# Normalising half of the input in a layout with channels on partitions, in place of transposing it

## The chip, the cores and the metric

The kernel runs on one core of a Trainium2 chip. The metric is the device time of one launch in microseconds (us); of several runs the median is given. Everything is float32; matrix products take a value as a rounded high part and the remainder (float32r tiles `hi` and `lo`) and add three products.

## The reference

One layer of an encoder over 2048 tokens of 1024 channels (D). Cut to what matters here:

```python
def _layernorm(x):
    xf = x.astype(jnp.float32)
    mu = jnp.mean(xf, axis=-1, keepdims=True)
    var = jnp.mean(jnp.square(xf - mu), axis=-1, keepdims=True)
    return (xf - mu) * lax.rsqrt(var + LN_EPS)

mod = c_act @ ada_w[l] + ada_b[l]
shift, scale, gate = jnp.split(mod, 3, axis=-1)
h = (_layernorm(x) * (1.0 + scale[:, None, :]) + shift[:, None, :]).astype(x.dtype)
proj = h @ w_in[l]                       # 1024 -> 9216 columns
y_hg = ...                               # gated recurrence (HGRN2), 8 heads, both directions
y_na = ...                               # 2-D neighbourhood attention, 16 heads, times a gate
y = jnp.concatenate([y_hg, y_na], axis=-1) @ w_out[l]
z = DEEPNORM_ALPHA * x + gate[:, None, :] * y
x = (_layernorm(z) * ln_g[l] + ln_b[l]).astype(x.dtype)
```

The matrix products need h with channels on the partitions; mean and variance of a token go over its channels.

## The kernel before

The tokens are cut in two halves of 1024 and each half in two groups of 512 (`GRP`): groups 0 and 1, then 2 and 3. h of one half lies in SBUF as 32 tiles `h` of 128 channels by 512 tokens (8 channel blocks `k`, two groups, high and low part). The h of the second half (`hs`, in DRAM) is prepared while the first half is worked on, and loaded over the first (`reload`, line 1429) when that is done.

The stages in order: `startup` (modulation sums, groups 0 and 1, first projections); `first_half` (neighbourhood attention of the first half, pair of heads by pair, in 8 rounds w); the recurrence, 16 rounds over heads and halves; the attention of the second half; the output projection with the final normalisation. In each stage `weave` mixes a generator of attention or recurrence steps with a generator `dense` of projection matmuls (`proj_mm`, line 272; `vproj`, line 285), so that TensorE has dense work between the dependent steps. A round of `first_half` holds, in TensorE's order: sums over values (line 1122), scores (1054, 1058), dense matmuls, transposes of the shares (1103), dense matmuls. VectorE and ScalarE do the softmax (1071 to 1081) between scores and transposes, and split each weight block into high and low part (842, 843).

In `first_half` TensorE's instructions keep the order in which the program writes them. Those of VectorE, ScalarE and SP are put in order by a planner at compile time, by priority and by when it estimates that operands and buffers are ready; each engine then runs its list strictly in that order, waiting where an operand is late. `pinned` keeps chosen instructions in the program's order among themselves (the statistics, line 212, are pinned). A tile of a tag has a fixed number of buffers, and a new tile waits for the last use of the old one: in this stage the tag `x` has 8 and the tag `s` (`short()`) 3.

Work on groups 2 and 3 (g = 0 and 1 in `first_half`) is put into `slots`, four for a round, which `natten_woven` calls between its steps. `rows` loads the 512 tokens as 8 tiles x of 128 tokens by 512 channels (line 199). `stats` takes mean and variance (212, 213) and the rate 1/sqrt(var + eps) (`rstd_of`, 184 to 191). `scale` normalises the tiles in place, half on ScalarE (226), half on VectorE (228). Each of 8 `piece`s then transposes four 128x128 blocks on TensorE into a PSUM tile (line 233, in `h_piece`), applies the modulation on ScalarE (235), takes high and low part on VectorE (239, 240) and stores both to `hs` (1345, 1346). The slots before and after:

```python
for g, i in ((0, 10), (1, 21)):
    slots[i].append((rows, g))
    slots[i + 1].append((stats, g))
    slots[i + 2].append((scale, g, 0))
    slots[i + 3].append((scale, g, 1))
    for k in range(KT):
        slots[i + 3 + k].append((piece, g, k))
```

All DMAs of this stage are issued by the queue of SP: weight blocks (line 832), key mirrors (987), value tiles (1000), bias tables (735, 736), stores (293, 1015, 1017, 1133), tables of the bias (718, 719). Earlier in the stage `gate_sum` stores 128 x 8 single elements to `gate_d` (line 178).

Of the kernel before, what the change touches and what calls it, by code (L numbers as in the profile page):

```python
# [10 lines left out]
F32 = mybir.dt.float32  # L11
F32R = mybir.dt.float32r
U32 = mybir.dt.uint32
AF = mybir.ActivationFunctionType
ALU = mybir.AluOpType
PSUM = bass.MemoryType.PSUM

D = 1024
SEQ = 2048
P = 128  # L20
KT = D // P
HALF = 1024
GRP = 512
# [14 lines left out]
def body(ctx: ExitStack, tc: tile.TileContext, t):  # L38
    nc = tc.nc
    dve, act, pool, pe = nc.vector, nc.scalar, nc.gpsimd, nc.tensor  # L40
    dma = nc.sync.dma_start
    x, out = t["x"], t["out"]

    cp = ctx.enter_context(tc.tile_pool(name="cp", bufs=1))
# [19 lines left out]
    def dram(name, shape, dt=F32):  # L64
        if name in t:
            return t[name]
        return nc.dram_tensor(name, shape, dt, kind="Internal").ap()
# [2 lines left out]
    yT = [yq[i // 4][:, i % 4, :] for i in range(16)]  # L70
    gate_d = dram("gate_d", (8, P))
    c_d = dram("c_d", (D,))
    hs = [dram(f"hs{k}", (P, 2, HALF)) for k in range(KT)]
    op_d = [dram(f"op{i}", (P, HALF)) for i in range(NHEAD)]
    qb_d = [dram(f"qb{i}", (P, HALF)) for i in range(NHEAD)]
# [15 lines left out]
    def nm(s):  # L91
        cnt[0] += 1
        return f"{s}_{cnt[0]}"

    def tl(tag, dt=F32, shape=None):
        if tag in cur["smap"]:
            tag = cur["smap"][tag]
            return sh.tile([P, 512], dt, tag=tag, name=nm(tag), bufs=SH[tag])
        return cur["pool"].tile([P, 512] if shape is None else shape, dt, tag=tag, name=nm(tag), bufs=cur["bufs"].get(tag, 1))

    def short(dt=F32):
        return tl("s", dt)

    def ps(tag="mx"):
        if tag == "pj":
            return pp.tile([P, 512], F32, tag=tag, name=nm("pj"))
        tag = cur["map"].get(tag, tag)
        return cur["psum"].tile([P, 512], F32, tag=tag, name=nm("ps"), bufs=cur["ps"][tag])
# [17 lines left out]
    shift = cp.tile([P, KT], F32, name="shift")  # L126
    scale1 = cp.tile([P, KT], F32, name="scale1")
# [65 lines left out]
    def x_load(g, pre=None):  # L193
        xs = []
        for i in range(4):
            xt = [pre if pre and i == 0 else tl("x"), tl("x")]
            r0 = g * GRP + i * P
            for a in range(2):
                dma(xt[a], x[r0:r0 + P, a * 512:(a + 1) * 512])
            xs.append(xt)  # L200
        return xs

    def x_stats(xs, pin=lambda x: x):
        mv = cp.tile([P, 4, 2], F32, tag="xmv", name=nm("xmv"), bufs=2)
        for i in range(4):
            x_stat(xs[i], mv[:, i, :], pin)
        return x_rate(mv)

    def x_stat(xt, mv, pin=lambda x: x):
        st = cp.tile([P, 2, 6], F32, tag="bnst", name=nm("bnst"), bufs=4)  # L210
        for a in range(2):
            pin(dve.bn_stats(st[:, a, :], xt[a]))
        dve.bn_aggr(mv, st)

    def x_rate(mv):
        r = cp.tile([P, 4], F32, tag="xr", name=nm("xr"), bufs=2)
        rstd_of(r, mv[:, :, 1])
        b = cp.tile([P, 4], F32, tag="xb", name=nm("xb"), bufs=2)
        dve.scalar_tensor_tensor(b, mv[:, :, 0], -1.0, r, op0=ALU.mult, op1=ALU.mult)
        return mv, r, b  # L220

    def x_scale(xs, how, a, on_act=2):
        mv, r, b = how
        for i in range(4):
            if i < on_act:
                act.activation(xs[i][a], xs[i][a], AF.Identity, scale=r[:, i:i + 1], bias=b[:, i:i + 1])
            else:
                dve.tensor_scalar(xs[i][a], xs[i][a], mv[:, i, 0:1], r[:, i:i + 1], op0=ALU.subtract, op1=ALU.mult)

    def h_piece(xs, k, hi, lo, early=False):  # L230
        pt = ps("hx")
        for i in range(4):
            pe.transpose(pt[:, i * P:(i + 1) * P], xs[i][k // 4][:, (k % 4) * P:(k % 4 + 1) * P], ident)
        tmp = short()
        act.activation(tmp, pt, AF.Identity, scale=scale1[:, k:k + 1], bias=shift[:, k:k + 1])
        if early:
            act.activation(hi, tmp, AF.Copy)  # L237
            return lambda: dve.tensor_tensor(lo, tmp, hi, op=ALU.subtract)
        dve.tensor_copy(hi, tmp)
        dve.tensor_tensor(lo, tmp, hi, op=ALU.subtract)  # L240
# [1073 lines left out]
    def first_half(raws, feed):  # L1314

        st = Prep(0, 0, raws)
        for n, _ in NCOL0:
            for g in range(2):
                st.piece(n, g)
        for _ in range(2):  # L1320
            feed.free(0)
        feed.tick()
        for j in (0, 1, 3):
            st.table("top", j)
        for _ in vproj(t["w_v"][0], nv_d[0], 0, feed):
            feed.tick()
        for c in range(3):
            st.v(c)
        pipe, xs = [], {}

        def rows(g):
            xs[g] = x_load(2 + g)

        how = {}

        def stats(g):
            how[g] = x_stats(xs[g], pinned)

        def scale(g, a):
            x_scale(xs[g], how[g], a)  # L1340

        def piece(g, k):
            a, b = short(F32R), short(F32R)
            h_piece(xs[g], k, a, b)
            dma(hs[k][:, 0, g * GRP:(g + 1) * GRP], a.bitcast(F32))
            dma(hs[k][:, 1, g * GRP:(g + 1) * GRP], b.bitcast(F32))

        slots = {i: [] for i in range(32)}
        slots[0].append((bias_pair, 1))
        for m in range(8):  # L1350
            slots[1 + m].append((gate_load, m))
            slots[3 + m].append((gate_sum, m))
        slots[5].append((lower_bounds,))
        for g, i in ((0, 10), (1, 21)):
            slots[i].append((rows, g))
            slots[i + 1].append((stats, g))
            slots[i + 2].append((scale, g, 0))
            slots[i + 3].append((scale, g, 1))
            for k in range(KT):
                slots[i + 3 + k].append((piece, g, k))  # L1360
        for u in range(2, 8):
            slots[4 * u - 6].append((bias_pair, u))
        for w in range(8):
            extra = {i: slots[4 * w + i] for i in range(4)}
            if w < 7:
                nxt = Prep(w + 1, 0, {n: [None, None] for n, _ in NCOL})
                dense, total, steps = first_stream(nxt, feed), NLEN + (0 if w % 2 == 0 else VLEN), 8
            else:
                nxt, dense, total, steps = None, hgrn_dense(0, 0, feed=feed), HTOT, 9
            r = weave(natten_woven(st, nxt, pipe, extra, w == 7), dense, total, steps)[1]  # L1370
            st = nxt
        return r
# [45 lines left out]
    with tc.manual_schedule(engines={mybir.EngineType.PE}):  # L1418
        with psum_phase("st", *SPS), phase("st", SB_, SMS), tc.manual_schedule(engines={getattr(mybir.EngineType, e) for e in ("PE", "SP", "Activation", "DVE")}):
            raws, feed = startup()  # L1420
        with psum_phase("n0", *NPS0), phase("n0", NB0, SM0):
            natten_init(4, 0)
            st = first_half(raws, feed)
# [232 lines left out]
def _arrays(inp):  # L1656
    import numpy as np

    f = {k: np.asarray(v) for k, v in inp.items()}
    a = {}  # L1660
    a["x"] = f["x"].reshape(SEQ, D)
    a["c"] = f["c"].reshape(P, KT)
    a["ada_w"] = f["ada_w"].reshape(D, 24, P).transpose(1, 2, 0)
    a["ada_b"] = f["ada_b"].reshape(24, P).T
    a["w_in"] = f["w_in"].reshape(KT, P, 72, P).transpose(2, 1, 0, 3).reshape(72, P, D)
    for n, c in (("w_i", 1024), ("w_v", 7168)):
        a[n] = f["w_in"].reshape(KT, P, 9216)[:, :, c:c + 1024].reshape(KT, P, 4, 256).transpose(2, 1, 0, 3).reshape(4, P, 2048)
    a["lb_logits"] = f["lb_logits"].reshape(16, P).T
    a["hg_norm_g"] = f["hg_norm_g"].reshape(P, 1)
    a["rpb"] = f["rpb"].reshape(2, 120, 31)  # L1670
    a["w_out"] = f["w_out"].reshape(2 * D, D)
    a["ln_g"] = f["ln_g"].reshape(1, D)
    a["ln_b"] = f["ln_b"].reshape(1, D)
    i, j = np.arange(P)[:, None] % 32, np.arange(32)[None, :]
    off, low, fw = i // 16 != j // 16, i < 16, i <= j
    a["mskd"] = np.stack([off, ~off & np.where(low, i >= j, fw), ~off & np.where(low, fw, i >= j)], 1).astype(np.float32)
    return {k: np.ascontiguousarray(v) for k, v in a.items()}
# [16 lines left out]
```

## Time and profile before

| | |
|---|---|
| median of 3 runs | 2611.91 us (2610.88 to 2613.2) |
| the profiled execution, its own time | 2614.25 us |
| span from its first to its last instruction | 2612.5 us |
| mean granted TensorE clock | 0.998 |
| instructions | 46055 |
| DMA traffic | 352.84 MB, 135 GB/s in the mean |

The profile is of one execution, taken by the hardware. PE is TensorE's matmuls and PEld its weight loads, which overlap them; DVE is VectorE, ACT ScalarE, POOL GpSimd, SP the engine whose queue (SPq) issues the DMAs. L233 is line 233. A row of instructions says what is written and read (`ps<-ident,x`: PSUM tile from identity and x), with buffer numbers left out. In the chain of work that ended last, each entry is a start, a length and a place; the engine named there had no slack in that time. The ends of matmuls are modelled, so lengths of neighbouring matmuls overlap; starts are measured.

### The profile page before, as it was taken

The page shows a single profiled execution, that of the slowest core. Times are in us where ns is not written, and L with a number is a line of the kernel's source. Part 1 is how long each engine was busy: PE and PEld are TensorE (multiplying, and loading weights), DVE is VectorE, ACT ScalarE, POOL GpSimd, SP SyncE. Part 2 cuts the span into 40 slices and gives each one's busy share as a digit, 9 for nine tenths or more (in the row PEclk, how much of TensorE's full clock was granted, in tenths as well). Part 3 has the DMA queues.
Part 4 walks back from the last instruction along what each step waited for, and adds up shares of the span by engine and source line. Part 5 has one row for each costly group of instructions (what it writes and reads, how often), then busy time and mean ns, then how long its engine had stood idle before and what let it go on. Part 6 is the DMA issues. An engine that isn't in the chain of part 4 may idle for free.

```text
span 2612.5 us, 46055 instructions
## 1 busy us (share of the span) xinstructions
PE 2565.1 (98%) x17328; PEld 2147.1 (82%) x17328; DVE 1756.1 (67%) x4351; ACT 1417.6 (54%) x2808; POOL 98.2 (4%) x119
## 2 busy tenths in 40 slices
PE   5999999999999999999999999999999999999998
PEld 3888888888888888888888888898888878888887
DVE  6446445478777778877787788537788888658443
ACT  4434444376666667666676666446666667531110
POOL 0000000000000000000000000000000000032221
PEclk9999999999999999999999999999999999999999
DMA  7555454212353347433233222454554445544331
GB/s 263 171 171 157 137 180 140 102 66 94 85 150 132 118 135 265 156 123 127 85 108 99 74 77 75 124 179 146 166 173 144 139 142 184 186 149 129 97 97 57
DMA packets 246318, 352.84 MB, mean 135 GB/s; under 512 B 31831, under 2 KB 122199, under 8 KB 245463
## 3 DMA queue, kind: packets, MB, share of 16 engines
q1 hardware_dynamic: 245807, 349.37, 42.3%
q8 instruction: 136, 2.23, 0.4%
q14 instruction: 87, 0.71, 0.1%
q10 hardware_dynamic: 288, 0.53, 0.1%
HBM read 266.21 MB, written 113.39 MB: 145 GB/s over the span
## 4 chain that ended last, share of the span: by engine, by line
PE 92%; DVE 3%; DMA 3%; ACT 2%; issue 1%; SPq 0%; DVEq 0%; ACTq 0%
PE pj L272 51%; PE pj L285 6%; PE ps L1510 4%; PE ps L1512 4%; PE ps L1511 4%; PE ps L1122 4%; PE ps L1103 3%; PE ps L486 2%; PE ps L1054 2%; PE ps L478 2%; PE ps L553 1%; PE ps L1058 1%; PE ps L577 1%; PE ps L579 1%; PE ps L525 1%; PE ps L654 1%
## 5 line engine op out<-in xcount | busy, mean ns | idle before, releaser
L272 PE MATMUL pj<-h,wh 128*128 128x512 f32 x4016 | 1278.1, 399 | 7.9 <-ACT h L237 5.6
L272 PEld LDWEIGHTS pj<-h,wh 128*128 128x128 f32 x4016 | 730.6, 188 | 163.7 <-issue 13.3
L272 PE MATMUL pj<-h,wl 128*128 128x512 f32 x2008 | 786.8, 392 | 0.0
L272 PEld LDWEIGHTS pj<-h,wl 128*128 128x128 f32 x2008 | 377.2, 188 | 82.6
L1076 ACT ACTIVATE pbuf<-pbuf,mx 128x480 f32<-128x480 f32 (+2 forms) x224 | 143.0, 639 | 136.8 <-DVE mx L1071 135.9
L285 PE MATMUL pj<-wh,h 128*128 128x256 f32 x1024 | 191.8, 286 | 0.9 <-ACT wh L842 0.7
L1071 DVE CUSTOM_DVE_ANT_1 pbuf<-ps,bias 128x480 f32<-128x480 f32 (+2 forms) x224 | 125.4, 589 | 95.0 <-PE ps L1058 80.3
L285 PEld LDWEIGHTS pj<-wh,h 128*128 128x128 f32 x1024 | 161.4, 191 | 4.5 <-issue 1.8
L263 DVE TENSOR_TENSOR wl<-wr,wh 128x512 fp32r<-128x512 f32 x192 | 131.2, 685 | 44.4 <-ACT wh L262 44.3
L262 ACT ACTIVATE wh<-wr 128x512 fp32r<-128x512 f32 x192 | 119.9, 625 | 60.0 <-PE pj L272 54.2
L285 PE MATMUL pj<-wl,h 128*128 128x256 f32 x512 | 144.9, 283 | 0.4 <-DVE wl L843 0.4
L1109 ACT ACTIVATE pt<-ps 128x512 f32<-128x512 f32 (+1 forms) x128 | 69.0, 539 | 86.2 <-PE ps L1103 84.8
L1107 DVE COPY pt<-ps 128x512 f32<-128x512 f32 (+1 forms) x128 | 78.9, 618 | 48.7 <-PE ps L1103 48.1
L790 ACT ACTIVATE e<-pj 128x512 f32<-128x512 f32 x100 | 59.2, 593 | 88.2 <-PE pj L272 84.4
L1483 ACT ACTIVATE yh<-yr 128x512 fp32r<-128x512 f32 x52 | 32.7, 629 | 133.5 <-PE ps L1511 114.6
L1103 PE MATMUL ps<-ident,pbuf 128*128 128x128 f32 x776 | 103.3, 273 | 0.0
L1103 PEld LDWEIGHTS ps<-ident,pbuf 128*128 128x128 f32 x776 | 90.9, 141 | 13.9 <-issue 0.2
L1566 DVE TENSOR_TENSOR vt<-ps,gt 128x512 f32<-128x512 f32 x24 | 16.5, 692 | 126.9 <-PE ps L1512 126.9
L843 DVE TENSOR_TENSOR wl<-wr,wh 128x512 fp32r<-128x512 f32 x68 | 46.8, 690 | 80.8 <-ACT wh L842 75.7
L1081 DVE TENSOR_SCALAR pbuf<-pbuf,mx 128x480 f32<-128x480 f32 (+2 forms) x224 | 95.9, 437 | 5.4
L285 PEld LDWEIGHTS pj<-wl,h 128*128 128x128 f32 x512 | 98.0, 191 | 1.4 <-DVE wl L843 0.6
L1122 PE MATMUL ps<-pt,V 128*64 128x128 f32 x1408 | 96.8, 277 | 1.0 <-DMA V<-nv 1.0
(278 smaller groups left out, 4687.9 us busy)
## 6 DMA issues: line engine op xcount, KB each, us to landing
wr<-in_w_in SPq DMA_DIRECT2D x276, 256.0 KB
nw<-nv SPq DMA_DIRECT2D x32, 512.0 KB
yr<-yq SPq DMA_DIRECT2D x60, 256.0 KB
emid<-tint SPq DMA_DIRECT2D x24, 480.0 KB
bias<-emid SPq DMA_DIRECT2D x24, 480.0 KB
V<-nw SPq DMA_DIRECT2D x40, 256.0 KB
bias<-ebot SPq DMA_DIRECT2D x24, 384.0 KB
x<-in_x SPq DMA_DIRECT2D x32, 256.0 KB
```

The source lines that it names most:

```text
L262: act.activation(hi, raw, AF.Copy)
L263: dve.tensor_tensor(lo, raw, hi, op=ALU.subtract)
L272: pe.matmul(pz, a, b, start=(k == 0 and n == 0), stop=(k == KT - 1 and n == 2))
L285: pe.matmul(pzs[tp][:, i * 256:(i + 1) * 256], a, b, start=(k == 0 and n == 0 and i == 0), stop=(k == KT - 1 and n == 2), skip_group_check ...
L1071: return dve.tensor_tensor_reduce(s[:, 0:nk].rearrange("p (r c) -> p r c", c=32), sc[:, 0:nk].rearrange("p (r c) -> p r c", c=32), bt[:, 0 ...
L1076: act.activation(s[:, 0:nk], s[:, 0:nk], AF.Exp, scale=-1.0, bias=mx[:, 0:1], accum_out=mx[:, 1:2])
L1081: dve.tensor_scalar(s[:, 0:nk], s[:, 0:nk], mx[:, 2:3], 1.0, op0=ALU.mult, op1=ALU.mult)
L1103: pe.transpose(ptp[:, c * P:(c + 1) * P], s[:, c * P:(c + 1) * P], ident)
L1122: pe.matmul(self.po[R][hs_, j * P:(j + 1) * P], self.st.V[c0 + c][:, j * P + hh * 64:j * P + hh * 64 + 64], pts[hh][:, c * P:(c + 1) * P], ...
L1510: pe.matmul(pz, yh[:, kk], wh, start=first, stop=False)
L1511: pe.matmul(pz, yh[:, kk], wl, start=False, stop=False)
L1512: pe.matmul(pz, yl[:, kk], wh, start=False, stop=last)
```

## The change

For groups 2 and 3 the host hands over a second copy of the last 1024 tokens of x, `x_t`, with channels on partitions. The rows are still loaded for the statistics. Mean and rate of the 512 tokens are copied into a small tile `mr`, stored to DRAM (`stat_d`), and loaded back spread over all partitions as two tiles of the tag x (`rates`). Each piece loads its 128 channels by 512 tokens as a tile z of the tag x, subtracts the spread means, multiplies by 1 + scale and the spread rates, adds the shift on ScalarE with rounding to the high part, and takes the low part on VectorE. `scale` and the transposes of these groups go. Groups 0 and 1 are as before.

```diff
+    stat_d = [dram(f"stat{g}", (2 * GRP,)) for g in range(2)]
...
-        how = {}
+        spread = {}
 
         def stats(g):
-            how[g] = x_stats(xs[g], pinned)
-
-        def scale(g, a):
-            x_scale(xs[g], how[g], a)
+            mv, r, _ = x_stats(xs[g], pinned)
+            mr = cp.tile([P, 2, 4], F32, tag="mr", name=nm("mr"), bufs=2)
+            dve.tensor_copy(mr[:, 0, :], mv[:, :, 0])
+            dve.tensor_copy(mr[:, 1, :], r)
+            dma(stat_d[g].rearrange("(s i p) -> p (s i)", p=P, i=4), mr.rearrange("p s i -> p (s i)"))
+
+        def rates(g):
+            spread[g] = [tl("x"), tl("x")]
+            for s in range(2):
+                dma(spread[g][s], stat_d[g][s * GRP:(s + 1) * GRP].rearrange("(o n) -> o n", o=1).to_broadcast([P, GRP]))
 
         def piece(g, k):
-            a, b = short(F32R), short(F32R)
-            h_piece(xs[g], k, a, b)
+            z, a, b = tl("x"), short(F32R), short(F32R)
+            dma(z, t["x_t"][k][:, g * GRP:(g + 1) * GRP])
+            dve.tensor_tensor(z, z, spread[g][0], op=ALU.subtract)
+            dve.scalar_tensor_tensor(z, z, scale1[:, k:k + 1], spread[g][1], op0=ALU.mult, op1=ALU.mult)
+            act.activation(a, z, AF.Identity, bias=shift[:, k:k + 1])
+            dve.scalar_tensor_tensor(b, z, shift[:, k:k + 1], a, op0=ALU.add, op1=ALU.subtract)
             dma(hs[k][:, 0, g * GRP:(g + 1) * GRP], a.bitcast(F32))
             dma(hs[k][:, 1, g * GRP:(g + 1) * GRP], b.bitcast(F32))
...
-            slots[i + 2].append((scale, g, 0))
-            slots[i + 3].append((scale, g, 1))
+            slots[i + 2].append((rates, g))
...
+    a["x_t"] = f["x"].reshape(SEQ, D)[HALF:].T.reshape(KT, P, HALF)
```

## The prediction

> **What bounds the kernel now.** I read the page's busy table first, then its chain of work that ended last. Columns of the busy table: time in us, share of the span, instructions.
>
> ```profile
> PE 2565.1 (98%) x17328; PEld 2147.1 (82%) x17328; DVE 1756.1 (67%) x4351; ACT 1417.6 (54%) x2808; POOL 98.2 (4%) x119
> ...
> PE 92%; DVE 3%; DMA 3%; ACT 2%; issue 1%; SPq 0%; DVEq 0%; ACTq 0%
> ```
>
> TensorE is busy for 98% of the span and is 92% of the chain. An average over stages isn't enough, so next comes the table of busy times by stretch, over the part that the change touches (264 us, where the rows of group 2 get their statistics, to 535 us, where the last piece of group 3 is stored). Five stretches; the first, the last and the sum:
>
> ```profile
> core 0: us, PE busy (x) PEld busy (x) DVE busy (x) ACT busy (x) POOL busy (x), PEclk, DMA share, GB/s
> 264.00:322.00 58.00, 58.00 (x370) 50.41 (x369) 21.74 (x50) 25.53 (x47) 0.51 (x2) 1.00 0.42 134
> ...
> 480.00:535.00 55.00, 55.00 (x300) 45.57 (x299) 19.14 (x46) 18.87 (x36) 0.63 (x2) 1.00 0.23 77
> sum 271.00, PE 271.00 PEld 229.64 DVE 123.63 ACT 118.31 POOL 3.43; mean PE 54.20 PEld 45.93 DVE 24.73 ACT 23.66 POOL 0.69
> ```
>
> TensorE is busy in all 271.00 us, at a granted clock of 1.00. VectorE idles for 271.00 - 123.63 = 147.4 us, ScalarE for 152.7 us. So here a microsecond of TensorE is a microsecond of the kernel, and work on the other engines is free as long as it delivers before TensorE asks.
>
> The third view is the chain in order of time (start, length, what), which shows the transposes of the pieces (line 233) as links of their own, four at a time. First a round of one attention head without a piece, then one with two:
>
> ```profile
> 212.00 1.46 PE ps L1122 x24
> ...
> 214.84 9.10 PE pj L272 x39
> ...
> 225.24 8.19 PE pj L272 x36
> 233.44 1.46 PE ps L1122 x24
> ...
> 319.78 1.46 PE ps L1122 x24
> ...
> 322.62 9.10 PE pj L272 x39
> 331.71 0.44 PE ps L233 x4
> ...
> 333.46 8.21 PE pj L272 x36
> 341.67 0.44 PE ps L233 x4
> 342.10 1.46 PE ps L1122 x24
> ```
>
> The two rounds hold the same other matmuls. Without pieces: 233.44 - 212.00 = 21.44 us; with two: 342.10 - 319.78 = 22.32 us. The difference is 0.88 us, 0.44 us a piece, and equals the links of line 233. That is the price of a piece on the path.
>
> **The change, part by part.** The instructions that go, or stay, from the answers on the tiles x, s and xt (duration in ns as min/median/max):
>
> ```profile
> L233 PE MATMUL ps<-ident,x x64: 270/272/273, 286.0 to 531.1; 128*128 128x128 f32 x64
> L199 SPq DMA_DIRECT2D x<-in_x x16: 327/402/799, 211.7 to 385.1; - x16
> ...
> L228 DVE TENSOR_SCALAR x<-x,xmv,xr x8: 537/540/544, 264.0 to 423.9; 128x512 f32<-128x512 f32 x8
> L226 ACT ACTIVATE x<-x,xb,xr x8: 798/804/817, 264.2 to 425.7; 128x512 f32<-128x512 f32 x8
> ```
> ```profile
> L235 ACT ACTIVATE s<-ps,shift,scale x16: 761/778/783, 286.6 to 532.0; 128x512 f32<-128x512 f32 x16
> L239 DVE CAST s<-s x16: 421/427/429, 287.4 to 532.8; 128x512 fp32r<-128x512 f32 x16
> ...
> L240 DVE TENSOR_TENSOR s<-s,s x16: 679/684/693, 287.9 to 534.0; 128x512 fp32r<-128x512 f32 x16
> ```
> ```profile
> L1567 DVE SCALAR_TENSOR_TENSOR xt<-xt,vt x32: 677/680/1792, 2332.2 to 2604.3; 128x512 f32<-128x512 f32 x32
> ...
> L1576 DVE SCALAR_TENSOR_TENSOR xt<-xt,bnr,sg x32: 744/750/755, 2339.3 to 2608.8; 128x512 f32<-128x512 f32 x32
> ```
>
> TensorE. The change removes 64 transposes, 16 pieces of four. Their medians sum to 64 x 0.272 = 17.4 us, but matmuls are pipelined and the next one starts before the last ends, so I take the links: 16 x 0.44 = 7.0 us. Nothing is added on TensorE.
>
> ScalarE. Removed: 8 x 0.804 (line 226) + 16 x 0.778 (line 235) = 18.9 us. Added: 16 shifts of a 128x512 tile, for which line 226, the same function from the same memory, is the nearest row: 16 x 0.804 = 12.9 us. Net -6.0 us, worth 0 on the path, since ScalarE has 152.7 us of idle time.
>
> VectorE. Removed: 16 x (0.427 + 0.684) + 8 x 0.540 = 22.1 us. Added for a piece: a subtraction at line 240's 0.684, and two scalar-tensor-tensor operations between 0.680 (line 1567) and 0.750 (line 1576); with a per-partition scalar like both of the new ones, 1576 is nearest. 16 x (0.684 + 2 x 0.750) = 34.9 us, and four copies of 128x4 at about 0.16 (the 128x1 reciprocal, line 1080, shown below) = 0.6 us. Net +13.4 us (11.2 at 0.680), against 147.4 us idle: 0 on the path by amount.
>
> Queues. All DMAs concerned are issued by SP; POOL's and ScalarE's queues get none. x is still loaded by rows for the statistics (line 199, 16 loads) and the stores to hs stay. Added for each group: one store of means and rates in 4-byte elements, two loads that spread them over the partitions, eight loads of z. The nearest rows, in the order SP issues them (start, length):
>
> ```profile
> 243.97 0.34 SPq L199 DMA_DIRECT2D x<-in_x  x1
> 244.67 0.63 SPq L178 DMA_DIRECT2D gate_d<-gatec  x1
> 245.35 0.57 SPq L199 DMA_DIRECT2D x<-in_x  x1
> ...
> 246.77 8.14 SPq L719 DMA_DIRECT2D tedge<-nb_d  x1
> ```
>
> The store of gatec has the same form, 128 x 8 elements of 4 bytes scattered. So 2 x 0.63 + 20 x (0.34 to 0.57) = 8 to 13 us of SP's 271. In bytes 16 x 256 KB + 4 x 256 KB = 5.2 MB; the first stretch moved 134 GB/s at a share of 0.42, 319 GB/s at full share, so 16 us of all engines, 0.06 on shares of 0.23 to 0.42 in the two stretches shown. Behind the small elements SP then hung for 8.14 us on one DMA while TensorE stayed full: queued weight loads outlast a stop of that length. I price the queue at 0, and at the stall below if that cover is gone.
>
> The new wait. Spread rows come only after a store and a load in sequence, and the trace has that pair once, at the start (chain, start and length), beside the softmax of one attention round and the transposes that need it:
>
> ```profile
> 5.22 5.82 DMA c_d<-cs
> 11.12 7.71 DMA cb<-c_d
> ```
> ```profile
> 349.21 0.16 DVE L1080 RECIPROCAL mx<-mx 128x1 f32<-128x1 f32 x1
> 349.40 0.40 DVE L1081 TENSOR_SCALAR pbuf<-pbuf,mx 128x352 f32<-128x352 f32 x1
> ```
> ```profile
> 353.21 0.60 PE L233 MATMUL ps<-ident,x 128*128 128x128 f32 x4
> 353.64 0.60 PE L1103 MATMUL ps<-ident,pbuf 128*128 128x128 f32 x4
> ```
>
> The pair takes 5.82 + 7.71 = 13.5 us. Nothing on TensorE asks for a piece in this stage: the h tiles are read back from hs much later (line 1429, below). But VectorE, ScalarE and SP work in order. If a piece's first subtraction is placed where the spread rows were expected sooner than they land, VectorE stands still, and behind it stand the softmax (lines 1071 to 1081) and the weight splits (line 843), for which TensorE waits. The cover in the round shown is 353.64 - (349.40 + 0.40) = 3.8 us, 3.4 once the 0.44 us of line 233 ahead of it is gone. A stop shorter than 3.4 us costs nothing, one of the full 13.5 us inside such a softmax 10.1 us; two groups, so 0 to 20 us. A gain from it is excluded: it is only a wait. I take 0, because the SP stop of 8.14 us went by unseen and because VectorE idles for more than half of the stage (147.4 of 271 us), so most places for a stop have nothing urgent behind them; the 20 us goes into the rivals.
>
> Pacing. Before, a piece ran when TensorE reached its transposes, 10 us apart in the round shown (331.71 and 341.67). Afterwards nothing of TensorE holds it, so eight pieces may run in a burst, limited by three buffers s (two for a piece, freed when the stores to hs land) and eight buffers x (two with the spread rows). The 8 x 2.18 = 17.5 us of VectorE work then lie between softmaxes; each instruction delays one by 0.75 us at most, inside 3.4 us.
>
> What is late next. After 553 us the stages are of the same kind:
>
> ```profile
> 553.00:1041.00 488.00, 485.09 (x3683) 410.35 (x3682) 376.46 (x966) 317.84 (x593) 0.59 (x6) 1.00 0.42 132
> 1041.00:1053.00 12.00, 12.00 (x67) 10.29 (x66) 7.38 (x23) 7.46 (x16) 0.00 (x0) 1.00 0.94 346
> ```
> ```profile
> L1429 SPq DMA_DIRECT2D h<-hs x32: 319/382/929, 991.6 to 1037.8; - x32
> ```
>
> TensorE idles for 2.9 us in 488, and just behind the reloads of h, with the DMA engines at 0.94, it is still full. The reloads and weights are released by TensorE's own progress, so they move forward with it: I carry the whole 7.0 us to the end.
>
> **The sum.** The profiled execution took 2614.25 us (span 2612.5 and 1.75 around it). -7.0 (TensorE) + 0 (ScalarE, VectorE, SP, DMA) = 2607.2 us. That execution lies 2.3 us above the median of the three runs, 2611.91, so on that scale 2604.9 us, 0.27% less. A difference under 0.2% (5.2 us) can't be told from no change in this kernel.
>
> The Trainium skill bears on the price of a transpose: "TensorE: Matmul & The Clock Gate", section "Part 4: PE-mode transpose", gives about 275 ns for one of 128x128 in a kernel's context. That agrees with this trace's 272 ns of one instruction, not with the 0.44 us in which four of them passed here; if 275 ns each came off the path, the estimate would be 17.6 us saved, 2594.3 us.
>
> **The rivals.**
> Busy time counts: the removed transposes free their 17.4 us, for instance because their weight loads hold up the next group too. For it: the 272 ns. Against it: the two rounds, 0.88 us apart with two pieces. 2611.9 - 17.4 = 2594.5 us. Chance 0.04.
>
> The gain is taken back in part: the planner orders VectorE, ScalarE and SP anew, and 2 to 9 us of small waits come up on TensorE, most likely one stop at each group's spread rows of 4.5 to 8 us, less the cover of 3.4. For it: 13.5 us of latency in a chain that was not there, and the burst. Against it: 8.14 us of SP stop without effect. 2607 to 2614, say 2610 us. Chance 0.26.
>
> The other side, slower by more than 0.2%: VectorE stops at the first subtraction of each group for the whole round trip, 13.5 us, with a softmax behind it: 2 x (13.5 - 3.4) = 20.2 us lost, 7.0 gained, 2625.1 us. It decides from 3.4 + 7.0 / 2 = 6.9 us of stop in each group (no gain), and brings slower from 9.5 us. For it: the pair of DMAs. Against it: the stop has to fall on a softmax with little cover, twice, and the z loads and spread rows may be expected late as well. Chance 0.10.
>
> The Trainium skill speaks for a short stop: "DMA: Bandwidth & Descriptors", section "Anatomy of one DMA — SWDGE (gpsimd) path", gives about 2 us fixed for a transfer, an estimate of 4 us for the pair and 0.6 us beyond the cover; these DMAs are issued by SP, and the trace's pair at 13.5 us speaks against it.
>
> **How the numbers follow.** The forecast, 2602 to 2606.7 us with 2604.9 the likeliest, has 0.60. Faster: 0.60 + 0.04 = 0.64; same: 0.26; slower: 0.10. The range reaches up over the partial loss to 2615 us, and down to 2600, for a VectorE that starts the next stage earlier; outside are the 17.4 us and most of the slower case, about 0.14.
>
> **What would show it.** The rows of line 233 from 264 us on are gone, and rounds that took 22.32 us take 21.44. TensorE stays full in the stage, and the last piece's part of the chain, before 535 us now, lies 7 us earlier. VectorE's busy time grows by 11 to 13 us, ScalarE's falls by about 6. The forecast is wrong if the list of waits shows TensorE waiting for VectorE's softmax or weight split with VectorE itself waiting for a DMA of a spread row or a z, or if a wait after 553 us has grown by several us.

## The result, and the profile after

The changed kernel takes 2643.27 us (median of 4 runs, 2638.91 to 2645.53) against 2612.36 us for the kernel before on the same chip: ratio 1.0115, 95% interval 1.0102 to 1.0127. It is slower by 31 us; 2604.9 us was predicted. Its profiled execution took 2642.9 us (span 2640.8, granted clock 0.991). In the changed file the lines from 72 to 1333 stand one further down: 272 is 273, 285 is 286, 1081 is 1082, 1103 is 1104, 1122 is 1123. The new ones: 1342 stores means and rates, 1347 loads the spread rows, 1351 loads z, 1352 subtracts, 1353 multiplies, 1354 adds the shift on ScalarE, 1355 takes the low part, 1356 and 1357 store to `hs`.

The busy table and the chain's shares:

```profile
PE 2563.6 (97%) x17264; PEld 2143.9 (81%) x17264; DVE 1768.2 (67%) x4363; ACT 1410.2 (53%) x2800; POOL 97.8 (4%) x119
...
PE 90%; DVE 4%; DMA 3%; ACT 2%; issue 1%; SPq 0%; DVEq 0%; ACTq 0%
```

TensorE has 64 matmuls fewer, VectorE 12.1 us more work, ScalarE 7.4 us less. The amounts are as forecast, but the span now has 77 us without a matmul (2640.8 - 2563.6), where it had 47. The busy times by stretch, in the same five stretches as before (columns as there; the first, the fourth, the last and the sum), say where:

```profile
264.00:322.00 58.00, 48.77 (x285) 42.02 (x284) 29.03 (x56) 20.45 (x40) 0.51 (x2) 0.91 0.71 217
...
426.00:480.00 54.00, 37.72 (x199) 30.11 (x199) 28.83 (x68) 17.31 (x35) 0.25 (x1) 0.84 0.64 192
480.00:535.00 55.00, 53.55 (x285) 43.45 (x284) 25.19 (x73) 22.49 (x51) 0.51 (x2) 1.00 0.24 80
sum 271.00, PE 244.03 PEld 204.06 DVE 129.42 ACT 104.14 POOL 2.79; mean PE 48.81 PEld 40.81 DVE 25.88 ACT 20.83 POOL 0.56
```

Where TensorE had been full for 271.00 us it idles for 27.0, nearly all of it in the stretches in which the pieces of group 2 and of group 3 begin; and there the granted clock falls to 0.91 and 0.84 in the mean. The list of TensorE's waits (from 130 us on; total, times, longest) names whom it waits for:

```profile
PE ps L1104 <- DVE pbuf L1082: 16.3, 2, 10.7
PE pj L273 <- ACT vt L292: 9.2, 1, 9.2
PE pj L273 <- issue: 4.0, 1, 4.0
...
PE ps L1104 <- DVE mx L1081: 1.5, 1, 1.5
```

Three of these waits are for the softmax on VectorE (lines 1081 and 1082), one is for the copying of a projection out of PSUM on ScalarE (line 292), and one, long after the stage, is for nothing that the profile shows. For group 2, the timelines of VectorE, ScalarE and TensorE (start, length, instruction, in brackets the idle time ahead of it and what ended that):

```profile
277.25 0.69 DVE L1352 TENSOR_TENSOR x<-x,x 128x512 f32<-128x512 f32 x1 [6.32 <-DMA x<-in_x_t]
...
280.93 0.72 ACT L1354 ACTIVATE s<-x,shift 128x512 fp32r<-128x512 f32 x1 [10.15 <-DVE x L1353]
...
286.85 0.72 ACT L1354 ACTIVATE s<-x,shift 128x512 fp32r<-128x512 f32 x1 [3.35 <-DMA hs<-s]
287.47 1.06 ACT L292 ACTIVATE vt<-pj 128x512 f32<-128x512 f32 x2
...
288.10 1.22 PE L273 MATMUL pj<-h,wh 128*128 128x512 f32 x2 [9.23 <-ACT vt L292]
```

VectorE stands 6.3 us for a z, ScalarE 10.2 us for VectorE, then 3.4 us for a buffer s that is free only when a store to `hs` has landed; behind it stand the copies of line 292, and TensorE needs their PSUM buffers. For group 3, the chain in order of time, and the rows of VectorE and TensorE behind it:

```profile
429.36 11.10 DMA stat<-mr
440.48 0.34 SPq L1347
...
442.38 5.18 DMA x<-in_x_t
...
453.34 6.81 DMA hs<-s
```
```profile
447.65 0.69 DVE L1352 TENSOR_TENSOR x<-x,x 128x512 f32<-128x512 f32 x1 [13.61 <-DMA x<-in_x_t]
...
450.32 0.52 DVE L1072 CUSTOM_DVE_ANT_1 pbuf<-ps,bias 128x352 f32<-128x352 f32 x1
...
457.65 1.51 PE L1104 MATMUL ps<-ident,pbuf 128*128 128x128 f32 x6 [10.67 <-DVE pbuf L1082]
...
464.78 1.51 PE L1104 MATMUL ps<-ident,pbuf 128*128 128x128 f32 x6 [5.61 <-DVE pbuf L1082]
```

SP waits for the store of means and rates, issues the spread loads and the z loads only then, and VectorE stands at the first subtraction for 13.6 us with a softmax behind it: TensorE had written the scores by 438 us, and their softmax begins on VectorE at 450.3 (line 1072). The second wait comes with the stores to `hs`.

To keep the stage apart from the rest I use one measure below: from the value sums of the round at 212.00 us before to those at 531.36, in the chain of the kernel before and of the changed one:

```profile
531.36 1.46 PE ps L1122 x24
```
```profile
209.77 1.46 PE ps L1123 x24
...
328.60 1.46 PE ps L1123 x24
...
350.03 1.46 PE ps L1123 x24
...
555.12 1.46 PE ps L1123 x24
```

Before 319.36 us, after 345.35: the stage is 26.0 us longer. A round without a stop takes 350.03 - 328.60 = 21.43 us, not the 22.32 of before, so the saving of 7.0 is in it, and the loss is 33 us: 27.0 of waits, and the remaining 6 behind them at a lower clock (the last section has the rows). Another 4.5 us come later, most of them in the wait of 4.0 us for nothing that the profile shows, at 749 us. (These two executions lie 28.3 us apart in their spans: -2.2 ahead of the stage, as the start varies from run to run, +26.0 in it, +4.5 behind it.)

### The profile page after: what moved, and what is told of

It is laid out like the page before. It is cut to its first block, busy times and chain, and to the rows that moved or that the text cites. A ratio compares the mean times of both kernels' runs of the same rounds, so it can differ in the third digit from the quotient of the medians.

```text
span 2640.8 us, 45927 instructions
## 1 busy us (share of the span) xinstructions
PE 2563.6 (97%) x17264; PEld 2143.9 (81%) x17264; DVE 1768.2 (67%) x4363; ACT 1410.2 (53%) x2800; POOL 97.8 (4%) x119
## 4 chain that ended last, share of the span: by engine, by line
PE 90%; DVE 4%; DMA 3%; ACT 2%; issue 1%; SPq 0%; DVEq 0%; ACTq 0%
PE pj L273 50%; PE pj L286 6%; PE ps L1520 4%; PE ps L1521 4%; PE ps L1522 4%; PE ps L1123 3%; PE ps L1104 3%; PE ps L487 2%; PE ps L1055 2%; PE ps L479 2%; PE ps L554 1%; PE ps L1059 1%; PE ps L578 1%; PE ps L580 1%; PE ps L526 1%; PE ps L655 1%
## 5 line engine op out<-in xcount | busy, mean ns | idle before, releaser
L264 DVE TENSOR_TENSOR wl<-wr,wh 128x512 fp32r<-128x512 f32 x192 | 131.4, 685 | 50.3 <-ACT wh L263 49.5
L1104 PE MATMUL ps<-ident,pbuf 128*128 128x128 f32 x776 | 104.9, 275 | 17.7 <-DVE pbuf L1082 16.3
L473 DVE TENSOR_TENSOR de<-e,de 128x512 f32<-128x512 f32 x64 | 44.2, 691 | 81.2 <-ACT de L472 81.2
```

Of the source, the lines that this page charges most:

```text
L264: dve.tensor_tensor(lo, raw, hi, op=ALU.subtract)
L1104: pe.transpose(ptp[:, c * P:(c + 1) * P], s[:, c * P:(c + 1) * P], ident)
```

## The experiments

My theory after the result: TensorE's transposes had spread the pieces over the rounds. Untied from it, the pieces stand early in the lists of VectorE, ScalarE and SP, and wherever one of their inputs or buffers is late, the engine stops with urgent work behind it. Rivals: the round trip of means and rates alone; the added DMAs or SP's queue; VectorE's added work.

**1. The pieces tied to TensorE again.** `paced` (a helper that the kernel has) lets an instruction wait for the TensorE instruction written last ahead of it.

```diff
-            dve.tensor_tensor(z, z, spread[g][0], op=ALU.subtract)
+            paced(dve.tensor_tensor(z, z, spread[g][0], op=ALU.subtract))
```

> The changed kernel with one edit: the first subtraction of each piece also waits for the last TensorE matmul ahead of its slot, so the planner can't place the pieces' VectorE and ScalarE work ahead of the slot. All DMAs stay. Theory (engines in order: VectorE and ScalarE stop at piece work placed before its operands land, with softmax and PSUM evacuations behind it): the waits of TensorE in the stage (27 us) go and the 7.0 us of the transposes come through, 2605 us (2602 to 2609). Rival contention (the 5.2 MB of added loads in bursts): the loads of z still go out early, so at least half of the loss stays, 2625 us or more. Rival queue (SP's waits for the store of means and rates): that wait stays, 2625 us or more.

Measured: 2617.15 us (11 runs), ratio 1.0018 (1.0009 to 1.0027), above the 2602 to 2609 that I expected. The stage takes 321.31 us: 24 of the 33 us are back. What is left are 6.1 us of TensorE waiting for line 1082 in four places, the longest behind this row of VectorE's timeline:

```profile
456.68 0.75 DVE L1355 SCALAR_TENSOR_TENSOR s<-x,shift,s 128x512 fp32r<-128x512 f32 x1 [9.12 <-DMA hs<-s]
```

A low part waited 9.1 us for a buffer s, of which there are three.

**2. Without the round trip.** The spread rows are read from a row that lies in DRAM from the start, so that h gets other values; the store of means and rates stays, and nothing waits for it.

```diff
-                dma(spread[g][s], stat_d[g][s * GRP:(s + 1) * GRP]...
+                dma(spread[g][s], c_d[s * GRP:(s + 1) * GRP]...
```

> The changed kernel, but the spread rows are loaded from a vector that is in DRAM since the start (c_d), so the normalisation uses wrong numbers; the store of means and rates stays, nobody waits for it. Theory (in order): the 13.6 us stop of VectorE before group 3's first subtraction goes, with the stall of 16.3 us behind it; stops at z and at the stores that free s stay in part: 2615 us (2605 to 2628). Rival contention: the bytes are the same, 2640 us. Rival queue: SP's wait of 15.8 us for the store goes, 2605 to 2615 us, so this run alone doesn't tell it from the theory.

Measured: 2647.95 us (4 runs), 1.0138 (1.0122 to 1.0154); stage 346.93 us. My expectation was wrong: without the round trip the loss is as large. VectorE's waits for a z have shrunk from 22.5 us in the changed kernel to 6.1; those for a buffer s have grown (ScalarE's from 21.4 us, VectorE's from 11.2):

```profile
ACT s L1354 <- DMA hs<-s: 23.7, 7, 9.5
DVE s L1355 <- DMA hs<-s: 18.3, 5, 9.2
```

The pieces begin earlier and stop at the buffers s instead.

**3. The DMAs alone.** All loads and stores of the change, none of its arithmetic: z is stored to `hs` as it is, so h is not normalised there.

```diff
-            dve.tensor_tensor(...)  # and the other three operations of a piece
-            dma(hs[k][:, 0, ...], a.bitcast(F32))
-            dma(hs[k][:, 1, ...], b.bitcast(F32))
+            for i in range(2):
+                dma(hs[k][:, i, g * GRP:(g + 1) * GRP], z)
```

> The changed kernel with the pieces' four VectorE and ScalarE instructions left out: z is loaded and stored to hs twice as it is, the spread rows are loaded and not read. So h of groups 2 and 3 is not normalised. All DMAs stay, and SP's wait for the store of means and rates. Theory (in order): nothing of the pieces stands in VectorE's or ScalarE's list, 2605 us (2602 to 2610). Rivals contention and queue: both causes are still there, 2625 us or more.

Measured: 2610.05 us (10 runs), 0.9992 (0.9983 to 1.0001); stage 312.28 us, 7.08 less than before, TensorE full. By themselves, the DMAs and SP's queue cost the stage nothing. The rest of the 7 us is lost later: 4.5 us of "issue" at 718 us.

**4. The arithmetic of the pieces on GpSimd**, in the same untied order and with all DMAs:

```diff
-            dve.tensor_tensor(z, z, spread[g][0], op=ALU.subtract)
...
+            pool.tensor_tensor(z, z, spread[g][0], op=ALU.subtract)
+            pool.tensor_tensor(z, z, spread[g][1], op=ALU.mult)
+            pool.tensor_scalar(z, z, scale1[:, k:k + 1], shift[:, k:k + 1], op0=ALU.mult, op1=ALU.add)
+            pool.tensor_copy(a, z)
+            pool.tensor_tensor(b, z, a, op=ALU.subtract)
```

> The changed kernel, not paced, with the arithmetic of the pieces (five instructions a piece) on GpSimd instead of VectorE and ScalarE. DMAs, bursts, buffers and the late spread rows are as in the changed kernel, so GpSimd stops where VectorE and ScalarE did, with nothing urgent behind it but fills of bias tables. Theory (engines in order): no wait of TensorE over 2 us in the stage, 2609 us (2605 to 2615). Rivals contention and SP queue: 2625 us or more.

Measured: 2609.59 us (10 runs), 0.9989 (0.9979 to 0.9998); stage 312.28 us. The stretches of group 2 and of group 3:

```profile
264.00:322.00 58.00, 58.00 (x360) 49.67 (x360) 28.72 (x47) 21.86 (x44) 38.09 (x34) 1.00 0.63 190
426.00:480.00 54.00, 54.00 (x290) 43.96 (x287) 32.84 (x74) 24.10 (x54) 35.31 (x33) 1.00 0.60 176
```

GpSimd works for 38 and 35 us, more than VectorE did on it, at a DMA share of 0.63 and 0.60 (0.71 and 0.64 in the changed kernel), and TensorE is full. GpSimd stands 71.4 us for z in this stage and 25.4 us for buffers s. Such waits on an engine that has nothing urgent in its list cost nothing.

**5. One buffer s for a piece instead of two**, the low part written over z; paced and unpaced.

```diff
-            z, a, b = tl("x"), short(F32R), short(F32R)
+            b, a = tl("x", F32R), short(F32R)
+            z = b.bitcast(F32)
```

> The paced kernel (first subtraction waits for TensorE's matmul ahead of its slot), and the low part is written over z instead of into a second buffer s, so a piece takes one of the three buffers s, not two. In the paced run VectorE stood 9.1 us at a low part, waiting for a buffer s whose store SP had issued 13 us after the data was ready. Theory (engines in order, with the buffers s as the link to SP): that stop and the 6.1 us of TensorE behind it go; the stage ends 7 to 8 us earlier than in the kernel before; at the end of the kernel 2609 us (2606 to 2612), since a stop of TensorE of 3 to 4.5 us near 720 us, seen in every changed kernel so far, stays. Rival (the stop came from the DMA engines, not the buffers): 2617 us as in the paced run.

> The changed kernel, not paced, with the low part written over z (one buffer s for a piece instead of two). Theory: of the stops, those on stores that free s shrink (VectorE 11.2 us, ScalarE 21.4 us in the changed kernel), those on spread rows and z (22.5 us) stay: 2628 us (2618 to 2638). If the buffers s carry nearly all: 2612 us. If they carry nothing: 2643 us.

Paced: 2608.73 us (11 runs), 0.9984 (0.9975 to 0.9992); stage 312.28 us, TensorE full in all 271 us. Unpaced: 2635.92 us (4 runs), 1.0089 (1.0075 to 1.0103); stage 341.04 us. Pacing and the buffer together give back the whole stage.

**6. Both late inputs taken away, unpaced** (edits 2 and 5 together):

> The changed kernel in its own order (no pacing), with both waits taken away at once: the spread rows are read from a row that lies in DRAM from the start, so nothing waits for the store of means and rates (values of h are then others), and the low part is written over z, so that a piece takes one buffer s and not two. Theory (each of the two waits alone stops VectorE or ScalarE for about as long, so that taking away one leaves the other): TensorE's waits in the stage fall from the 27 us of the changed kernel and the 24 to 27 us of the two single edits to under 8 us; 2607 to 2615 us. Rival (the z loads themselves, or the order that the planner gives, stop VectorE): 2630 us or more, with the subtraction waiting for a z.

Measured: 2648.25 us (4 runs), 1.0137 (1.0123 to 1.0151); stage 349.28 us. My expectation fell, the rival's held. VectorE's row and SP's:

```profile
486.31 0.69 DVE L1353 TENSOR_TENSOR x<-x,x 128x512 f32<-128x512 f32 x1 [12.65 <-DMA x<-in_x_t]
```
```profile
481.05 1.08 SPq L1352 DMA_DIRECT2D x<-in_x_t  x2
```

Now the last two z of the group are late: SP issues their loads at 481 us, behind stores to `hs`, and VectorE has stood at the subtraction (line 1353 here) since 473.7. Each late input that is removed lets the pieces run up to the next one.

**7. The round trip in the kernel before.** Its pieces and transposes stay; added are the store, the spread loads, and one subtraction on VectorE for each group that reads both spread rows and whose result nobody uses.

```diff
+            slots[i + 2].append((rates, g))
+            slots[i + 3].append((touch, g))   # dve.tensor_tensor(spread[g][0], spread[g][0], spread[g][1], op=ALU.subtract)
```

> The kernel before, with its transposes, plus only the new round trip: each group's means and rates are stored, spread over the partitions by two loads, and one subtraction of 128x512 on VectorE reads the spread rows; its result is used by nothing. Theory (what costs is where the stop stands in VectorE's order, and in the changed kernel the pieces stand early because nothing of TensorE holds them back): here the subtraction stands later in VectorE's order, for group 2 behind the first piece's low part and a weight split, for group 3 directly ahead of a softmax; the rows have landed or are a few us away, and TensorE loses 0 to 6 us: 2612 to 2619 us. Rival (the round trip of 13.5 us is itself the price, as the prediction's other side had it, 10.1 us for each group): 2628 us or more, with TensorE waiting for line 1082 or for a weight split.

Measured: 2610.69 us (10 runs), 0.9994 (0.9985 to 1.0004); stage 319.35 us. VectorE's wait for the spread rows, and the list of TensorE's waits from 130 to 800 us, complete:

```profile
DVE x L1353 <- DMA x<-stat: 8.8, 2, 7.2
```
```profile
PE ps L487 <- ACT ke L481: 1.6, 1, 1.6
PE ps L578 <- ACT gt L385: 1.3, 1, 1.3
```

VectorE does stop at the spread rows, for 7.2 and 1.6 us, and TensorE does not notice (both of its waits lie behind the stage). The stops end at 339.7 and 474.2 us, later than those at the first subtractions of the changed kernel (277.3 and 447.7). Behind the longer one stands a weight split, behind the shorter one a softmax. So the round trip costs nothing where its reader stands late; a long stop ahead of a softmax is not tried by this run.

**8. The price of a transpose.** The kernel before with the 64 transposes of these groups issued twice:

> The kernel before with each of the 64 transposes of groups 2 and 3 done twice into the same place (the second overwrites the first with the same). It prices what their removal is worth. By the links of the chain (0.44 us for four): +7.0 us, 2619 us (2617 to 2621). By the busy time of one (0.272 us): +17.4 us, 2630 us.

Measured: 2625.66 us (5 runs), 1.0052 (1.0039 to 1.0064); stage 326.05 us, 6.69 more than before. In the chain a piece's eight transposes pass in twice the 0.44 us:

```profile
332.13 0.87 PE ps L234 x8
```

The profiled execution's span is 10.3 us longer than before (2622.8 against 2612.5); 3.4 us of this are again a wait for "issue", at 728 to 731 us.

**9. The late stop.** Wherever it appears, it comes at the same place of TensorE's list counted from the start, up to a multiple of 128 matmuls, each with its weight load: 4270 to 4272 matmul records lie ahead of it in the changed kernel and in edits 1 to 6, 4399 with the doubled transposes. A packet of 16 KB of the instruction queue (q8) begins 2.2 to 2.4 us before TensorE goes on, and in the changed kernel the DMA engines' share is 0.96 from 735 to 750 us. So my theory: instructions come in blocks of 256, and one is late when its fetch meets busy DMA engines. The change takes away 64 matmuls and 64 loads, half a block. Padding at the start, whose results nobody reads, shifts the blocks:

```diff
+        pad = ps("hx")
+        for i in range(64):   # first run; 32 in the others
+            pe.matmul(pad[0:32, i:i + 1], ident[:, 0:32], ident[:, 0:1], start=True, stop=True, skip_group_check=True)
```

First on the paced kernel of edit 5, with 64:

> The kernel of run e9_paced_bz with 64 matmuls of one column put at TensorE's start, where it waits for x anyway, so that every later instruction of TensorE has as many ahead of it as in the kernel before. Theory on the stop near 720 us (TensorE's instructions are fetched in blocks by the same DMA engines; the block falls due while a large copy saturates them, and 128 instructions fewer moved it there): the stop goes, 2605 us (2602 to 2607), with no wait over 1.7 us between 553 and 1000 us. Rival (the stop comes from the earlier stage or from something else moved in time): the stop stays, 2609 us.

Measured: 2607.21 us (11 runs), 0.9978 (0.9969 to 0.9987); the stop is still there, 3.2 us at 715 us. The trace shows why: each of these lines became two matmuls and two loads, so 64 lines are a whole block and shift nothing. It also speaks against a part of the theory: from 704 to 714 us, up to this stop and into it, the DMA engines' share is 0.19 (0.96 in the same stretch of the kernel without padding), and the stop is as long. Full DMA engines are not what the stops have in common. With 32, half a block:

> The paced kernel whose low part is written over z, with 32 one-column matmuls on TensorE at the start, whose results nobody reads. In the padded run before this one 64 such lines gave 128 matmuls and 128 weight loads, 256 instructions, and the late stop stayed where it was; 32 lines give 64 and 64. Theory (the late stop is a block of 256 TensorE instructions that arrives late through busy DMA engines): the block's edge moves by half a block to about 701 us and 728 us, both outside the stretch of busy DMA engines (703 to 723 us); no stop of 2 us or more between 690 and 760 us, and a time 3 to 4 us below the same kernel without padding: 2605 us (2602 to 2607). Rival (the stop belongs to this place in the program, for instance to the data that its matmuls read): the stop of about 3 us stays at 715 us and the time is 2608.7 us.

Measured: 2602.30 us (5 runs, 2601.81 to 2605.91), 0.9963 (0.9951 to 0.9976); stage 312.30 us. The same place in the chain of the paced kernel without padding and with it:

```profile
708.99 3.43 PE pj L273 x15
712.42 2.92 issue
715.34 8.01 PE pj L273 x27
```
```profile
708.44 9.55 PE pj L273 x42
```

The stop is gone: the 42 matmuls take 9.55 us, not 14.36. Then the same 32 lines in the kernel before, which had no such stop:

> The kernel before with the same 32 one-column matmuls at the start and nothing else changed. Theory (late block of instructions): the block's edge, at 707 and 736 us before, moves to about 698 and 722 us, the second inside the stretch in which the DMA engines are full (711 to 731 us); a stop of 2 to 4.5 us for nothing that the profile shows appears near 722 us, with a lower clock behind it: 2615 to 2617 us, ratio 1.001 to 1.002. Rival (the stop comes from what the pieces changed): no stop, 2612 to 2613 us, ratio 1.000.

Measured: 2618.48 us (11 runs), 1.0023 (1.0014 to 1.0032); stage 319.43 us as before. Chain, and the queues between 718 and 726 us (packets, MB, share):

```profile
718.82 3.43 PE pj L272 x15
722.25 3.24 issue
725.48 8.01 PE pj L272 x27
```
```profile
q1 hardware_dynamic: 520, 0.69, 104.4%
q8 instruction: 1, 0.02, 0.8%
```

The stop was made at the expected place, in a program otherwise unchanged. Last, the padding in the changed kernel:

> The changed kernel with the 32 one-column matmuls at the start and nothing else changed. Theory (the loss of the changed kernel is two things that add up: the stops at the pieces, and the late block of instructions at 749 us): the stop of 4.0 us and the low clock behind it go, the waits of 27 us in the stage stay: 2637 to 2640 us, 4 to 5 us below the changed kernel's 2643. Rival (the late stop is a consequence of the delay in the stage, and moves with it): 2643 us, with a stop of 3 us or more that the profile names no releaser for.

Measured: 2637.96 us (4 runs), 1.0100 (1.0085 to 1.0115): 5.3 us below the changed kernel, no late stop, the waits of the stage much as they were (15.7 and 11.6 us, against 16.3 and 9.2). The two losses are separate, and the account closes: 26 us in the stage, 5 us at the late block.

That instructions come in blocks of 256 is concluded from these positions. It fits that the changed kernel has 135 packets of q8 for 2 x 17264 matmuls and loads, 256 for each; no row names the queue's contents. What holds the block up was not tried, and stays open. The traces leave one candidate: line 760 (759 before) fills 1.5 MB of `ebot` in DRAM from one row of 1 KB, in 1536 packets and some 25 us, and it is paced by TensorE as well. In the eleven traces with the stop, the late packet of q8 begins 18.5 to 20.5 us after this filling began. In the four without it, one packet comes ahead of the filling and the next only at its end, within 0.5 us.

## Why the prediction was wrong

Both signs of being wrong that the prediction named came true: TensorE waits for the softmax while VectorE waits for a z, and a wait after 553 us has grown.

- **TensorE, -7.0 us: right.** Five kernels without a stop in the stage (3, 4, 5 paced, and its two padded versions in 9) have a stage of 312.28 to 312.30 us, 7.06 to 7.08 less than before. That is 0.44 us for a piece, not the 64 x 0.272 us of single instructions; "busy time counts" and, with it, 275 ns each are refuted as the price on the path.
- **VectorE, ScalarE, queues by amount: right.** +12.1 us was measured on VectorE (11 to 13 forecast), -7.4 on ScalarE (-6 forecast); the DMAs alone cost the stage nothing (3).
- **"Pacing" is the step that failed.** It saw that nothing of TensorE would hold the pieces, and priced the burst by the length of its instructions, 0.75 us each. A piece's instruction can also stand for a late operand or buffer: 13.6 us for a z in the changed kernel, 5 us for a buffer s there and 9 us in experiment 1. With the pieces tied to TensorE again 24 us come back (1), with the low part over z all 33 (5).
- **"The new wait", taken as 0, was mis-sized for the changed kernel, and for the wrong reason.** Its first reason, that a stop of SP goes unseen, does not carry over to a stop of VectorE or ScalarE. Its second, that VectorE idles for more than half of the stage, counts time and not place: the planner put the first subtractions ahead of work that TensorE asked for next. Only VectorE was named as the blocked engine; 9.2 of the 27 us are ScalarE's copies out of PSUM. The buffers s were mentioned and not priced.
- **"The other side"** had the sign, and one of the stops as it came: in group 3 VectorE stood 13.6 us at the first subtraction, behind the round trip and ahead of a softmax. It did not have the cause of the whole loss: without the round trip the pieces stop elsewhere and nothing comes back (2), and where its rows are read later it costs nothing (7). Its 2625.1 us are 18 us too low. The waits were 27.0 us and not 20.2, part of them on ScalarE, and the 6 us of low clock and the 5 us at the late block were not in it.
- **"What is late next": wrong.** Not all 7.0 us reach the end. The changed kernel, and each version of it without half a block of padding, stops for 2.1 to 4.5 us at a block of instructions, since 64 matmuls and 64 loads fewer move the blocks by half their length. The instruction queue was not in view.
- The Trainium skill ("DMA: Bandwidth & Descriptors", section "Anatomy of one DMA — SWDGE (gpsimd) path") gives about 2 us fixed for a transfer on GpSimd's path. Here, issued by SP, the store of 1024 single elements took 11.1 us in the chain, with the two table loads of lines 719 and 720 issued right behind it; the measured number decides, though by experiments 2 and 7 this store alone is not what costs.

## What to carry to other kernels

When a change removes the link that paced side work, price the pieces by the latest of their inputs and buffers and by what stands behind them on every engine that they use, not by the engine's idle time; tie them to the bottleneck engine again, or give them to an engine with nothing urgent. Removing one late input of an untied burst only lets it run to the next. Before believing a gain or loss of a few us, look whether a stop for "issue" has come or gone: here 128 instructions of TensorE more or fewer, at the start of the kernel, were worth 5 to 6 us, and the change with pacing, one buffer and padding takes 2602.3 us, 0.37% less than before.

## What the runs showed of the hardware

- TensorE can stop for 2.1 to 4.5 us for nothing that its waits show, at a fixed place of its instruction list. The places lie 128 matmuls with their loads apart, and half of that as padding removed the stop (2608.7 to 2602.3 us) or made it (2612.6 to 2618.5 us). A late block of instructions is the reading of this; the DMA share ahead of the stop was 0.96 in one trace and 0.19 in another.
- A wait of TensorE can cost more than its length, by the clock. Behind the 9.2 us wait of group 2 in the changed kernel, 21 matmuls of line 273 take 7.85 us (0.37 us each), where 36 take 8.19 (0.23 each) in an undisturbed round:

```profile
288.10 7.85 PE pj L273 x21
...
341.84 8.19 PE pj L273 x36
```

The stretch of group 3's two waits, with 1.74 us of matmuls in 13 and a granted clock of 0.50:

```profile
452.00:465.00 13.00, 1.74 (x7) 1.39 (x8) 11.36 (x26) 7.05 (x15) 0.25 (x1) 0.50 0.58 198
```

So 27 us of waits became 33 us of lost time. Not every wait has this effect: behind the stop of 3.15 us in experiment 6, at 754.7 us, 28 matmuls take 6.64 us (0.24 each).
